# A mixture-of-experts tail: token list written in parts and loaded from POOL's queue, expert tables read two ahead, a tile of its own for the second norm

## Chip, cores and metric

One core of a Trainium2 chip. The metric is device time in microseconds (us) of the whole kernel, the median of three runs. The engines are TensorE (PE; its weight loads are PEld), VectorE (DVE), ScalarE (ACT), GpSimd (POOL) and SyncE (SP), each with its own instruction queue, worked through in order. SP and POOL also issue the DMA transfers; all indirect ones (rows gathered or scattered by a list of indices) are POOL's.

## The reference

One layer of a decoder with 2048 tokens of 1024 channels in fp32. First a token mixer (two kinds of attention, gates, an output projection) and a layer norm, which the change does not touch. Then the mixture of experts:

```python
idx, gates = group_route(x2d, w_router, router_bias)   # one of 8 groups of 4 experts; top 2 in it
h = jax.nn.silu(xb @ w_gate[e]) * (xb @ w_up[e])       # per expert: 1024 -> 512
yb = h @ w_down[e]                                     # 512 -> 1024
y = segment_sum(yb * gate, token)                      # two experts per token
out = layer_norm(alpha * x + y, ln2_g, ln2_b)          # the second norm
```

## The kernel before

**Up to the experts.** The mixer writes the normed rows x1 and alpha times x1 (into `scr["y"]`) to DRAM. `route` (L600) gives each token its group and two experts and scatters (token, gate) pairs into a table `scr["tab"]`, one stretch of rows for each expert (L669). `sort_experts` orders the 32 experts so that each of 32 static slots knows how many rows it must hold: wide slots hold 128 + 64 rows, narrow ones 128. `MIX` (L32) is that order by (group rank, expert rank in the group), `BIG` says which slots are wide (14 of 32), `STAGE` which of five parts of `MIX` a slot is in.

**One expert** (`experts`, L946, loop L972). In iteration i the code emits, in this order: `start(i + 1)`, i.e. `prep` of the next expert; the loads of the second norm that fall due; `gate_up(i)`; `hidden(i)`; the norms of the loaded rows; `down(i - 1)`.
- `prep` (L802) reads the expert's table with SP (L808, and L810 for the 64 rows), gathers the token rows `xg` with POOL (L815; tag Z, three buffers), transposes them on TensorE (L823, L831) and splits them into a high and a low part on ScalarE and VectorE (L83, L84). The wide part's result, `x3`, lies in one of two halves of a tile of tag R.
- `weights` (L836) loads 1 MB with SP (L839; staging tag V, five buffers) and splits it (L83, L84) into `wh` and `wl`, tag X. Each expert has four such loads for gate and up and two for down.
- `gate_up` (L847), `hidden` (L872) and `down` (L900) are the three steps of matmuls. `down` scales by the gate (L915), makes the wide part's `y3` on ScalarE and VectorE (L923, L924; tag Y, two buffers) and adds the rows into `scr["y"]` by an indirect DMA that accumulates, on POOL (L927).

**The token list.** `token_list` (L717), emitted at i = 1, works out for each token its place in an order by group and scatters the 2048 token numbers there, sixteen indirect DMAs of 128 rows of 8 bytes on POOL (L756). SP then loads the list into `lst` (L763).

**The second norm.** A 128-token block of that list can be normed once the groups it holds have been summed. Blocks 0 to 12 are normed inside the loop: `when` (L967) gives blocks 0 to 2 to iterations 10, 12, 14, blocks 3 to 6 to 18, 20, 22, 24, blocks 7 to 10 to 26 to 29 and blocks 11 and 12 to 30 and 31. `norm_load` (L992) gathers the rows with POOL (L996) into `fz`, tag Y, shared with `y3`; `norm` (L1013) computes mean and variance (L1019, L425), the inverse root with three Newton steps (`rstd`, L405; products L416, L420), and L1022 and L1023; `norm_rows` stores by POOL (L1008). The last three blocks follow the loop (L988), each with a Newton chain of its own; the first of them takes its passes on ScalarE.

**What sets the order.** The tile framework's planner orders each engine's queue by readiness in its own timing model and by emission order; it puts a wait where a buffer or a result is needed. An engine never passes a waiting instruction, so the table read of SP stands behind its weight loads, and POOL's gathers, y sums, norm loads and stores stand in one line.

Of the kernel before, what the change touches and what calls it, by code (L numbers as in the profile page):

```python
# [11 lines left out]
F32 = mybir.dt.float32  # L12
# [41 lines left out]
class Layer:  # L54
# [662 lines left out]
    def token_list(self):  # L717
# [27 lines left out]
        g = self.b([128, 4, 16])  # L745
# [8 lines left out]
        prev = []  # L754
        for t in range(16):
            st = nc.gpsimd.indirect_dma_start(  # L756
                out=self.scr["list"], out_offset=bass.IndirectOffsetOnAxis(ap=dst[:, t:t + 1], axis=0),
                in_=self.tok[:, t, :], in_offset=None)
            for p in prev:
                self.tc.declare_no_dep(st.ins, p.ins, reason="rows of another token")  # L760
            prev.append(st)
        self.lst = self.c("lst", [128, 16, 2], I32, "binT")
        nc.sync.dma_start(self.lst, self.scr["list"].rearrange("(b p) v -> p b v", p=128))  # L763
# [38 lines left out]
    def prep(self, e, row, big):  # L802
# [8 lines left out]
        S["tb"] = tb  # L811
        xr = []
# [13 lines left out]
        if big:  # L826
            x3 = self.x3s[:, self.turn % 2]
            self.turn += 1
            pt = self.p("aT", [128, KD, 64])
            for k in range(KD):  # L830
                nc.tensor.transpose(pt[:, k, :], xr[1][:, k * 128:(k + 1) * 128], self.ident[0:64, 0:64])  # L831
            self.split(pt, x3[:, :, 0, :], x3[:, :, 1, :])
            S["x3"] = x3
# [112 lines left out]
    def experts(self):  # L946
# [5 lines left out]
        def start(i, e=None):  # L952
            e = expert(i) if e is None else e
            S = self.prep(e, e * ROWS + ROWS, BIG[i])
            S["slot"] = i
            return S

        self.gb = self.norm_consts(2)
        self.x3s, self.turn = self.t("R", [128, 2, KD, 2, 64], F32R, "x3"), 0
        e = expert(0)  # L960
        w = [self.weights("w_gu", e, 0, after=self.fence(self.scats[-1]))]
        cur, nxt, old = start(0, e), start(1), None
        w.append(self.weights("w_gu", e, 1, after=nxt["read"], sync=False))
        w.append(self.weights("w_gu", e, 2, after=self.fence(nxt["gather"])))
        cur["w"] = w
        self.sums, self.reads, self.rows = [], [], []
# [5 lines left out]
        for i in range(32):  # L972
            if i:
                nxt = start(i + 1) if i < 31 else None
            rows = [self.norm_load(b, q) for q, b in when.get(i, ())]
            self.gate_up(cur)
            self.hidden(cur)
            for r in rows:
                self.norm_rows(r, "D")
            if old is not None:  # L980
                self.down(old)
            old, cur = cur, nxt
            if i == 1:
# [20 lines left out]
    def norm_rows(self, r, how):  # L1004

        z, at = r
        self.norm(z, how)
# [5 lines left out]
    def norm(self, x, how):  # L1013
        nc = self.nc
        g, b = self.gb[:, 0, :], self.gb[:, 1, :]
        if how == "D":
            st = self.small([128, 2, 6])
            for h in range(2):
                nc.vector.bn_stats(st[:, h, :], x[:, h * 512:(h + 1) * 512])  # L1019
            mean, var = self.moments(st)  # L1020
            rs = self.rstd(var)
            nc.vector.scalar_tensor_tensor(x, x, mean, g, op0=OP.subtract, op1=OP.mult)  # L1022
            nc.vector.scalar_tensor_tensor(x, x, rs, b, op0=OP.mult, op1=OP.add)  # L1023
            return
        y = self.t("F", [128, D], F32, "fy")
        sm = self.small([128, 5])
        nc.scalar.activation(y, x, AF.Copy, accum_out=sm[:, 0:1])
        nc.vector.tensor_scalar(sm[:, 1:2], sm[:, 0:1], -1.0 / D, None, op0=OP.mult)
        nc.scalar.activation(y, x, AF.Square, bias=sm[:, 1:2], accum_out=sm[:, 2:3])
        nc.vector.tensor_scalar(sm[:, 3:4], sm[:, 2:3], 1.0 / D, None, op0=OP.mult)  # L1030
        rs = self.rstd(sm[:, 3:4])
        nc.vector.tensor_tensor(sm[:, 4:5], sm[:, 1:2], rs, op=OP.mult)
        nc.scalar.activation(x, x, AF.Identity, bias=sm[:, 4:5], scale=rs)
        nc.vector.tensor_tensor(x, x, g, op=OP.mult)  # L1034
        nc.vector.tensor_tensor(x, x, b, op=OP.add)  # L1035

    def finish(self, out):
# [11 lines left out]
        with tc.For_i(0, again, 1) as i:  # L1049
            z = self.t("Y", [128, D], F32, "fz")  # L1050
            nc.sync.dma_start(z, self.scr["y"][ds(i * 128, 128)])
            self.norm(z, "D")
# [133 lines left out]
```

## Time and profile before

| | |
|---|---|
| median of 3 runs | 2571.21 us (2567.74 to 2575.26) |
| the profiled execution | 2575.09 us |
| its span, first to last instruction | 2573.1 us |
| mean granted TensorE clock | 0.974 |
| TensorE matmul busy | 94% of the span |
| VectorE / ScalarE / POOL busy | 73% / 55% / 34% |

The clock is a share of 2.4 GHz. A line of a timeline gives start, duration, engine, line of the kernel, operation, output and inputs; in brackets stands how long the engine had been idle before it and what ended that.

### The profile page before, as it was taken

How to read it: one execution, taken by the hardware profiler on the slowest of the kernel's cores; microseconds unless marked ns; L12 is line 12 of the kernel's file. 1: busy time of each engine (PE TensorE's matmuls, PEld its weight loads, DVE VectorE, ACT ScalarE, POOL GpSimd, SP SyncE). 2: the span in 40 equal slices, each digit the busy share in tenths (PEclk: the TensorE clock that was granted, in tenths of full speed). 3: DMA queues.
4: the chain of work that ended last, by engine and by line, in shares of the span. 5: the costliest groups of instructions: out<-in, count | busy, mean ns of one | idle time of the engine just before them, and what ended most of it. 6: DMA issues, size and time to landing. Idle time of an engine off the chain costs nothing. (4 is left out here: it accounts for less than half of the span.)

```text
span 2573.1 us, 37165 instructions
## 1 busy us (share of the span) xinstructions
PE 2419.9 (94%) x12706; PEld 2032.2 (79%) x12706; DVE 1867.2 (73%) x3065; ACT 1419.6 (55%) x2388; POOL 869.0 (34%) x942
## 2 busy tenths in 40 slices
PE   8999899999999999999999999949979989999992
PEld 7888778988888888888878888737768878877871
DVE  4554757657777877778867878766767877897893
ACT  3442636457776766777732222225656666666661
POOL 0220424234444444444410312232532452332522
PEclk9999999999999999999999999969989999999996
DMA  7747576454443423238274554258699999999993
GB/s 255 202 145 224 158 207 191 154 157 137 138 136 103 152 85 97 86 90 286 92 249 161 189 164 148 92 171 299 220 338 325 354 312 328 325 363 340 349 308 86
DMA packets 173055, 528.52 MB, mean 205 GB/s; under 512 B 28592, under 2 KB 53168, under 8 KB 146096
## 3 DMA queue, kind: packets, MB, share of 16 engines
q1 hardware_dynamic: 155264, 468.38, 53.9%
q0 software_dynamic: 17600, 57.73, 8.5%
q8 instruction: 103, 1.69, 0.3%
q14 instruction: 88, 0.72, 0.1%
HBM read 404.88 MB, written 121.73 MB: 205 GB/s over the span
## 5 line engine op out<-in xcount | busy, mean ns | idle before, releaser
L84 DVE TENSOR_TENSOR wl<-ws,wh 128x2048 fp32r<-128x2048 f32 (+2 forms) x250 | 507.5, 2039 | 148.2 <-ACT wh L83 110.1
L83 ACT ACTIVATE wh<-ws 128x2048 fp32r<-128x2048 f32 (+2 forms) x250 | 424.2, 1713 | 133.6 <-PE pz L865 53.3
L348 POOL TENSOR_TENSOR s<-s,keep 128x512 f32<-128x512 f32 (+2 forms) x320 | 315.3, 991 | 402.4 <-DVE keep L346 401.3
L160 PE MATMUL pmm<-xh,wh 128*128 128x512 f32 x912 | 364.2, 400 | 6.0 <-ACT xh L83 5.8
L161 PE MATMUL pmm<-xl,wh 128*128 128x512 f32 x912 | 362.9, 398 | 0.2 <-DVE xl L84 0.2
L162 PE MATMUL pmm<-xh,wl 128*128 128x512 f32 x912 | 362.9, 398 | 0.2 <-DVE wl L84 0.2
L346 DVE TENSOR_TENSOR_SCAN keep<-pz,keep,s 128x512 f32<-128x512 f32 x192 | 244.9, 1279 | 57.5 <-ACT pz L341 57.0
L84 DVE TENSOR_TENSOR at<-paT,at 128x512 fp32r<-128x512 f32 (+3 forms) x384 | 225.2, 614 | 76.7 <-ACT at L83 74.4
L83 ACT ACTIVATE at<-paT 128x512 fp32r<-128x512 f32 (+3 forms) x384 | 191.4, 541 | 110.8 <-PE paT L351 104.6
L279 POOL TENSOR_SCALAR sw<-sw,st 128x256 f32<-128x256 f32 (+1 forms) x128 | 124.1, 985 | 361.2 <-DVE st L277 163.8
L927 POOL DMA_INDIRECT scr_y<-y,tb x46 | 120.3, 2615 | 289.8 <-ACT y L915 241.7
L160 PEld LDWEIGHTS pmm<-xh,wh 128*128 128x128 f32 x912 | 173.4, 190 | 37.9 <-ACT xh L83 6.2
L340 ACT ACTIVATE s<-pz 128x512 f32<-128x512 f32 (+2 forms) x320 | 172.1, 538 | 54.8 <-PE pz L244 45.2
L162 PEld LDWEIGHTS pmm<-xh,wl 128*128 128x128 f32 x912 | 173.1, 190 | 33.2 <-DVE wl L84 0.5
L161 PEld LDWEIGHTS pmm<-xl,wh 128*128 128x128 f32 x912 | 173.1, 190 | 32.5 <-DVE xl L84 1.0
L859 PE MATMUL pmm<-wh,xt 128*128 128x512 f32 x512 | 178.3, 403 | 4.5 <-ACT h L875 3.0
L243 PE MATMUL pz<-kt,qt 128*128 128x256 f32 (+3 forms) x448 | 164.7, 378 | 13.6 <-DVE keep L346 5.7
L869 PE MATMUL pmm<-wl,xt 128*128 128x512 f32 x512 | 174.5, 400 | 2.5 <-DVE wl L84 2.5
L861 PE MATMUL pmm<-wh,xt 128*128 128x512 f32 x512 | 174.1, 398 | 0.0
L341 ACT ACTIVATE pz<-pz 128x512 f32<-128x512 f32 (+2 forms) x320 | 173.7, 543 | 0.0
L358 PEld LDWEIGHTS po<-at,vt 128*128 128x128 f32 x1152 | 159.9, 190 | 16.4 <-ACT at L83 1.6
L358 PE MATMUL po<-at,vt 128*128 128x256 f32 x1152 | 165.5, 283 | 2.2 <-ACT at L83 1.2
(295 smaller groups left out, 5352.2 us busy)
## 6 DMA issues: line engine op xcount, KB each, us to landing
ws<-in_w_gu SPq DMA_DIRECT2D x128, 1024.0 KB, 8.1
ws<-in_w_dn SPq DMA_DIRECT2D x64, 1024.0 KB, 8.8
ws<-in_w_in SPq DMA_DIRECT2D x57, 512.0 KB, 4.7
qt<-scr_qkh SPq DMA_DIRECT2D x64, 256.0 KB, 5.6
qt<-scr_qkl SPq DMA_DIRECT2D x64, 256.0 KB, 6.5
scr_gate<-sg SPq DMA_DIRECT2D x64, 256.0 KB, 3.1
bs<-in_w_br SPq DMA_DIRECT2D x32, 512.0 KB, 4.0
gl<-scr_gate SPq DMA_DIRECT2D x64, 256.0 KB, 3.8
```

What stands on the lines that cost most here:

```text
L83: nc.scalar.activation(hi, src, AF.Copy)
L84: (lo_eng or nc.vector).tensor_tensor(lo, src, hi, op=OP.subtract)
L160: ins.append(nc.tensor.matmul(ps, wh[:, k, :], h, start=k == 0, stop=False))
L161: ins.append(nc.tensor.matmul(ps, wh[:, k, :], l, start=False, stop=False))
L162: ins.append(nc.tensor.matmul(ps, wl[:, k, :], h, start=False, stop=k == KD - 1))
L341: nc.scalar.activation(z[:, :w], z[:, :w], AF.Sigmoid, scale=-0.125)
L346: nc.vector.tensor_tensor_scan(kp[:, k0:k0 + w][:, ::-1], z[:, :w][:, ::-1], s[:, :w], init, op0=OP.mult, op1=OP.bypass)
L348: nc.gpsimd.tensor_tensor(s[:, :w], s[:, :w], kp[:, k0 + 1:k0 + w + 1], op=OP.mult)
L358: nc.tensor.matmul(o, vt[:, 4 * c + i, :], at[:, r, i], start=(c == top and i == nbs[1] - 1 and r == 0), stop=(c == 0 and i == 0 and r == 1))
L859: nc.tensor.matmul(ps[u], xh, wh[:, kk, u, :], start=a, stop=False)
L861: nc.tensor.matmul(ps[u], xl, wh[:, kk, u, :], start=False, stop=False)
L869: nc.tensor.matmul(ps[u], xh, wl[:, kk, u, :], start=False, stop=z)
```

## The change

The order of stages 1 and 2 alternates groups strictly. The list is scattered in four parts, in iterations 2 to 5, from a tile of its own (`where`, in the place of `bwr`), and loaded by POOL. The table reads of `prep` become a function `read` that runs two experts ahead. `x3` moves to tag Y, and `fz` of the loop becomes one tile that is used by all blocks (tag R, where `x3` was). `norm` takes a list of blocks and makes one Newton chain for all of them; the last three blocks go through it together and are stored after it.

```diff
-       ((1, 0), (7, 0), (7, 1), (1, 1), (7, 2), (1, 2), (1, 3), (7, 3)),
-       ((2, 0), (5, 1), (2, 1), (2, 2), (5, 0), (2, 3), (5, 2), (5, 3)),
+       ((1, 0), (7, 0), (1, 1), (7, 1), (1, 2), (7, 2), (1, 3), (7, 3)),
+       ((2, 0), (5, 1), (2, 1), (5, 2), (5, 0), (2, 2), (5, 3), (2, 3)),
...
-        g = self.b([128, 4, 16])
+        g = self.c("where", [128, 3, 16], F32, "bwr")
...
-        prev = []
-        for t in range(16):
+        self.where, self.lists = dst, []
+
+    def token_rows(self, t0):
+        dst, prev = self.where, self.lists
+        for t in range(t0, t0 + 4):
             st = nc.gpsimd.indirect_dma_start(
...
+        if t0 < 12:
+            return
         self.lst = self.c("lst", [128, 16, 2], I32, "binT")
-        nc.sync.dma_start(self.lst, self.scr["list"].rearrange("(b p) v -> p b v", p=128))
+        nc.gpsimd.dma_start(self.lst, self.scr["list"].rearrange("(b p) v -> p b v", p=128))
...
-            x3 = self.x3s[:, self.turn % 2]
-            self.turn += 1
+            x3 = self.t("Y", [128, KD, 2, 64], F32R, "x3")
...
-        self.x3s, self.turn = self.t("R", [128, 2, KD, 2, 64], F32R, "x3"), 0
+        self.fz = self.t("R", [128, D], F32, "fz")
         e = expert(0)
...
-        cur, nxt, old = start(0, e), start(1), None
+        cur, nxt, old = start(0, read(0, e)), start(1, read(1)), None
...
+        far = read(2)
...
             if i:
-                nxt = start(i + 1) if i < 31 else None
+                nxt = start(i + 1, far) if i < 31 else None
+                far = read(i + 2) if i < 30 else None
...
             if i == 1:
                 self.token_list()
+            if 2 <= i < 6:
+                self.token_rows(4 * (i - 2))
...
-        for r, how in zip(rows, "ADD"):
-            self.norm_rows(r, how)
+        self.norm([z for z, _ in rows], "ADD")
+        for r in rows:
+            self.norm_store(r)
...
-    def norm_load(self, b, stage, tag="Y"):
-        z = self.t(tag, [128, D], F32, "fz")
+    def norm_load(self, b, stage, tag=None):
+        z = self.t(tag, [128, D], F32, "fz") if tag else self.fz
...
+        mv = self.small([128, n, 2])
+        for i, (x, how) in enumerate(zip(xs, hows)):
...
+        rs = self.rstd(mv[:, :, 1], n)
+        for i, (x, how) in enumerate(zip(xs, hows)):
...
```

## Rows read from the trace of the kernel before

**Rows 1.** Busy time by stretch: PE, PEld, DVE, ACT, POOL, PEclk, DMA share, GB/s

```profile
1840.00:1860.00 20.00, 20.00 (x91) 16.51 (x90) 19.12 (x14) 15.01 (x14) 18.17 (x7) 1.00 0.54 159
1860.00:1880.00 20.00, 7.18 (x34) 5.08 (x33) 0.00 (x0) 1.54 (x1) 6.66 (x6) 0.83 0.94 222
...
1900.00:1950.00 50.00, 50.00 (x238) 40.79 (x237) 36.50 (x28) 34.40 (x34) 18.21 (x8) 1.00 0.88 315
```

**Rows 2.** TensorE's timeline, expert stage: the instructions behind its longer idle stretches

```profile
1868.21 0.63 PE L823 MATMUL paT<-ident,xg 128*128 128x128 f32 x4 [3.51 <-DMA xg<-scr_x,tb]
...
1880.43 0.80 PE L912 MATMUL po<-wh,ht 128*128 128x512 f32 x1 [9.74 <-ACT wh L83]
...
1882.75 0.80 PE L914 MATMUL po<-wl,ht 128*128 128x512 f32 x1 [1.10 <-DVE wl L84]
...
2115.15 0.87 PE L823 MATMUL paT<-ident,xg 128*128 128x128 f32 x3 [6.04 <-DMA xg<-scr_x,tb]
...
2307.40 1.22 PE L869 MATMUL pmm<-wl,xt 128*128 128x512 f32 x2 [2.46 <-DVE wl L84]
...
2523.41 0.77 PE L912 MATMUL po<-wh,ht 128*128 128x512 f32 x1 [7.62 <-DVE y L924]
```

**Rows 3.** Busy time by stretch, columns as in rows 1, behind the longest gap

```profile
1880.00:1884.00 4.00, 2.47 (x5) 1.56 (x6) 3.40 (x2) 3.42 (x5) 1.73 (x1) 0.50 1.02 424
1884.00:1888.00 4.00, 4.00 (x15) 3.06 (x15) 4.00 (x4) 3.94 (x4) 0.00 (x0) 0.65 1.00 416
```

**Rows 4.** POOL's timeline: the first, a long and the last list scatter, and the next gather

```profile
1826.37 0.99 POOL L756 DMA_INDIRECT scr_list<-tok,B  x1 [11.72 <-DVE C L777]
...
1842.73 7.49 POOL L756 DMA_INDIRECT scr_list<-tok,B  x1 [0.30 <-issue]
...
1857.57 2.56 POOL L756 DMA_INDIRECT scr_list<-tok,B  x1 [0.30 <-issue]
1860.43 0.97 POOL L815 DMA_INDIRECT xg<-scr_x,tb  x1 [0.30 <-PE pmm L861]
```

**Rows 5.** SP's waits after 1700 us (total, times, longest), and its timeline

```profile
SPq L763 <- DMA scr_list<-tok,B: 18.7, 1, 18.7
...
1864.27 0.39 SPq L763 DMA_DIRECT2D lst<-scr_list  x1
```

**Rows 6.** POOL's timeline: a wide expert's two gathers, 128 rows and 64 rows

```profile
1780.99 0.94 POOL L815 DMA_INDIRECT xg<-scr_x,tb  x1 [23.19 <-DMA tb<-scr_tab]
1782.34 0.90 POOL L815 DMA_INDIRECT xg<-scr_x,tb  x1 [0.41 <-PE paT L889]
```

**Rows 7.** VectorE's timeline beside the long list scatter

```profile
1842.70 6.67 DVE L84 TENSOR_TENSOR wl<-ws,wh 128x2048 fp32r<-128x2048 f32 x3
```

**Rows 8.** POOL's waits after 1700 us: total, times, longest

```profile
POOL xg L815 <- DMA tb<-scr_tab: 85.3, 9, 23.2
```

**Rows 9.** ScalarE's timeline near the end

```profile
2521.95 1.08 ACT L923 ACTIVATE y<-po 64x512 f32<-64x512 f32 x2 [8.36 <-DMA out<-fz,lst]
```

**Rows 10.** POOL's timeline: loads and stores of norm blocks 4, 7 and 11

```profile
2225.42 1.30 POOL L996 DMA_INDIRECT fz<-scr_y,lst  x1 [7.58 <-DMA out<-fz,lst]
...
2357.02 2.61 POOL L996 DMA_INDIRECT fz<-scr_y,lst  x1 [6.42 <-DMA scr_y<-y,tb]
...
2399.75 2.78 POOL L1008 DMA_INDIRECT out<-fz,lst  x1 [0.80 <-DMA tb<-scr_tab]
...
2494.82 3.20 POOL L996 DMA_INDIRECT fz<-scr_y,lst  x1 [6.67 <-issue]
...
2517.12 0.97 POOL L1008 DMA_INDIRECT out<-fz,lst  x1 [0.73 <-DVE sm L416]
```

**Rows 11.** DMA issues after 1700 us: times, median us from issue to landing

```profile
out<-fz,lst POOLq DMA_INDIRECT x16, 10.4
```

**Rows 12.** POOL's timeline: its last instruction

```profile
2561.69 0.95 POOL L1008 DMA_INDIRECT out<-fz,lst  x1 [0.30 <-issue]
```

**Rows 13.** VectorE's groups after 2540 us: busy, mean ns

```profile
L416 DVE SCALAR_TENSOR_TENSOR sm<-sm 128x1 f32<-128x1 f32 x9 | 1.8, 213 | 0.0
```

More of the change, by code (lines that the diff above doesn't have):

```diff
@@ L753, in token_list @@
         v.tensor_reduce(self.late[:, 0:1], late[0:1], axis=AX.X, op=OP.add)
-        prev = []
-        for t in range(16):
+        self.where, self.lists = dst, []
+    def token_rows(self, t0):
+        nc = self.nc
+        dst, prev = self.where, self.lists
+        for t in range(t0, t0 + 4):
             st = nc.gpsimd.indirect_dma_start(
@@ L800, in overflow_list, with read @@
         v.tensor_copy(self.ove, po)
-    def prep(self, e, row, big):
+    def read(self, e, row, big):
         nc = self.nc
@@ L811, in prep @@
         S["tb"] = tb
+        return S
+    def prep(self, e, row, big, S=None):
+        nc = self.nc
+        S = self.read(e, row, big) if S is None else S
+        tb = S["tb"]
         xr = []
@@ L950, in expert, with read, start @@
             return nc.sync.value_load(self.eid[0:1, i:i + 1], min_val=0, max_val=31)
-        def start(i, e=None):
+        def read(i, e=None):
             e = expert(i) if e is None else e
-            S = self.prep(e, e * ROWS + ROWS, BIG[i])
+            S = self.read(e, e * ROWS + ROWS, BIG[i])
             S["slot"] = i
             return S
+        def start(i, S):
+            return self.prep(None, None, BIG[i], S)
         self.gb = self.norm_consts(2)
-        self.x3s, self.turn = self.t("R", [128, 2, KD, 2, 64], F32R, "x3"), 0
+        self.fz = self.t("R", [128, D], F32, "fz")
         e = expert(0)
         w = [self.weights("w_gu", e, 0, after=self.fence(self.scats[-1]))]
-        cur, nxt, old = start(0, e), start(1), None
+        cur, nxt, old = start(0, read(0, e)), start(1, read(1)), None
         w.append(self.weights("w_gu", e, 1, after=nxt["read"], sync=False))
@@ L1004, in norm_rows, with norm_store @@
     def norm_rows(self, r, how):
+        self.norm([r[0]], how)
+        self.norm_store(r)
+    def norm_store(self, r):
         z, at = r
-        self.norm(z, how)
         st = self.nc.gpsimd.indirect_dma_start(out=self.io["out"], out_offset=at, in_=z, in_offset=None)
@@ L1011, in norm_rows, with norm @@
         self.rows.append(st)
-    def norm(self, x, how):
+    def norm(self, xs, hows):
         nc = self.nc
+        n = len(xs)
         g, b = self.gb[:, 0, :], self.gb[:, 1, :]
[L1016 to L1035, printed above, removed]
@@ new lines, in norm @@
+        mv = self.small([128, n, 2])
+        for i, (x, how) in enumerate(zip(xs, hows)):
+            if how == "D":
+                st = self.small([128, 2, 6])
+                for h in range(2):
+                    nc.vector.bn_stats(st[:, h, :], x[:, h * 512:(h + 1) * 512])
+                nc.vector.bn_aggr(mv[:, i], st)
+            else:
+                y = self.t("F", [128, D], F32, "fy")
+                sm = self.small([128, 3])
+                nc.scalar.activation(y, x, AF.Copy, accum_out=sm[:, 0:1])
+                nc.vector.tensor_scalar(sm[:, 1:2], sm[:, 0:1], -1.0 / D, None, op0=OP.mult)
+                nc.scalar.activation(y, x, AF.Square, bias=sm[:, 1:2], accum_out=sm[:, 2:3])
+                nc.vector.tensor_scalar(mv[:, i], sm[:, 0:3:2], 1.0 / D, None, op0=OP.mult)
@@ new lines, in norm @@
+        rs = self.rstd(mv[:, :, 1], n)
+        for i, (x, how) in enumerate(zip(xs, hows)):
+            m, q = mv[:, i, 0:1], rs[:, i:i + 1]
+            if how == "D":
+                nc.vector.scalar_tensor_tensor(x, x, m, g, op0=OP.subtract, op1=OP.mult)
+                nc.vector.scalar_tensor_tensor(x, x, q, b, op0=OP.mult, op1=OP.add)
+            else:
+                nm = self.small([128, 1])
+                nc.vector.scalar_tensor_tensor(nm, m, -1.0, q, op0=OP.mult, op1=OP.mult)
+                nc.scalar.activation(x, x, AF.Identity, bias=nm, scale=q)
+                nc.vector.tensor_tensor(x, x, g, op=OP.mult)
+                nc.vector.tensor_tensor(x, x, b, op=OP.add)
@@ L1051, in finish @@
             nc.sync.dma_start(z, self.scr["y"][ds(i * 128, 128)])
-            self.norm(z, "D")
+            self.norm([z], "D")
             nc.sync.dma_start(out[ds(i * 128, 128)], z)
```

## The prediction

> **What bounds the kernel now.** I read the windows by stretch first. From 1900 us on TensorE is busy without a break at full clock (50.00 of 50 us), with the 16 DMA engines at 0.88 and POOL at 18.21 of 50 [rows 1]. So the expert stage is bound by TensorE wherever nothing stops it, and what the change can win is TensorE's idle time and the tail behind it. The exception is 1860 to 1880 us, where TensorE works 7.18 of 20 us; just before it, the DMA engines fall to 0.54 and POOL is busy 18.17 of 20 us [rows 1].
>
> Next, TensorE's own timeline gives its idle stretches with what ended them [rows 2]: 3.51 us for a late token gather, 9.74 us for a down-projection weight, 1.10 us for its low half, later 6.04 us for another late gather, 2.46 us for a weight half, and 7.62 us near the end for y3, the small block's output. After an idle stretch the clock is granted at 1.2 GHz: 0.50 in the four us after the 9.74 us gap and 0.65 in the next four [rows 3]. Busy time times missing clock gives the price: 2.47 x 0.50 + 4.00 x 0.35 = 2.6 us.
>
> POOL's timeline then says why the gather was late. The sixteen scatters that write the token list run in one row from 1826.37 to 1857.57 + 2.56 = 1860.13, 33.8 us, and the gather goes out right behind, at 1860.43 [rows 4]. SP's rows say why the weight was late: its load of the list waited 18.7 us for the scatters and went out at 1864.27, 4.1 us after the last of them had been issued; all weight loads stood behind it [rows 5], and the 9.74 us are TensorE's wait for such a weight. Two queues thus gave one stall.
>
> **The change part by part.**
>
> *List in four parts, list load on POOL.* Removed from the path: 3.51 + 9.74 + 1.10 = 14.35 us idle and 2.6 us of slow clock, 17.0 us. The scatters stay, 33.8/16 = 2.1 us each, 8.4 us for a part. POOL has some 32 of 50 us free [rows 1], which hides them; without that cover they would again stand ahead of a gather. The load itself is late to nobody: the first reader of the list comes iterations later. But POOL now waits for the last scatters, 4.1 us, and makes the load's 2048 pieces of 8 bytes. No row shows such a load on POOL. The nearest rows: SP issued it in 0.39 us [rows 5]; a scatter of 128 such pieces, the first, takes 0.99 us, sixteen like it 15.8 us [rows 4]; a gather takes 0.94 us for 128 rows and 0.90 for 64 [rows 6], so 64 pieces more cost 0.04 us and 2048 pieces 0.9 + 1.3 = 2.2 us. I take 2.2 us, because the two gathers measure the very slope that is asked for; the ends are 0.39 and 15.8. Behind the waiting load stand gathers and y scatters. Their cover: a POOL row of 33.8 us delayed TensorE by just 3.51 us, so 30.3 us were hidden; 8.4 + 4.1 + 2.2 = 14.7 us fit. Cost nothing.
>
> One scatter took 7.49 us, not 0.99. It starts at 1842.73 [rows 4] as VectorE starts three wide subtractions in a row (1842.70, 6.67 us [rows 7]) and ends 0.85 us after them: POOL stood still while VectorE worked, and lost 6.5 us. A load on POOL that meets such a run loses as much: 14.7 + 6.5 = 21.2 us still fit into 30.3. [...]
>
> *Tables two experts ahead.* POOL waited 85.3 us for tables [rows 8], but TensorE's rows blame a gather only for the 3.51 us, counted above, and the 6.04 us. Whether a table or POOL's order made the second late, its row does not say. Gain between 0 and 6.04 + 2.6 = 8.6 us; I take 0, since POOL has other waits in the same places. SP issues as many table reads as before, one expert earlier.
>
> *Y tiles and the second norm's own tile.* At the end ScalarE waited 8.36 us for y3's buffer, until an output store of the norm had landed [rows 9]; that is TensorE's 7.62 us. With the norm out of Y this goes, and so does the slow clock behind it, which I put at the 2.6 us worked out above: 10.2 us. The two x3 buffers join y3 in Y; as wide experts now alternate with narrow ones, an x3 takes the buffer of the y3 two experts back, and no wait is added.
>
> The norm pays for it: with one tile, block b+1's load waits on POOL until block b's store has landed. From a load to the store behind it POOL's rows take 22.3 us (2494.82 to 2517.12) at best and 42.7 us (2357.02 to 2399.75) at worst [rows 10], and a store lands in 10.4 us [rows 11]: a block every 32.7 to 53.1 us, where blocks 7 to 12 come one an expert. From 2357.02 six blocks at the best pace have the last store out at 2357.0 + 5 x 32.7 + 22.3 = 2542.8 us. Before, the last store of all went out at 2561.69 [rows 12]; 10.2 us less for y3 and 1.2 for the batched norm below put it at 2550.3 on the same clock (the 17.0 us move both). So the chain fits by 7.5 us, and I add the 2.9 us by which one landing of 10.4 exceeds that. A wait like it, 7.58 us on POOL [rows 10], left TensorE without a gap, so in mid-stage I count none. The ends are 0 and the rival below.
>
> *One Newton chain for the last three blocks.* The nine Newton products took 1.8 us of VectorE [rows 13]; three chains become one, so two thirds go, 1.2 us, of 0 to 1.8. The batch must wait for all three loads; the chain already ends with the third block, so this adds nothing.
>
> *Order.* Each expert costs the same. Experts 13 to 15 are now three narrow ones in a row, and weights are asked for fastest there. The one such run of before ended in the 2.46 us gap [rows 2]. Bounds 0 and 2.46 + 2.6 = 5.1 us; I take 2.5, the gap as it stands. Sums into the same rows now alternate; no row shows POOL waiting for such a sum, so nothing.
>
> **Sum.** -17.0 - 10.2 - 1.2 + 2.9 + 2.5 = -23.0 us. The profiled execution took 2575.1 us (span 2573.1), 3.9 us above the median, so it would come to 2552; from the median of 2571.2 I forecast 2548 us. A measurement of this kernel can tell about 0.3%, 7.7 us, from no change.
>
> **Rivals.**
> *The second late gather goes too*: tables no longer hold POOL up. For it, the 85.3 us [rows 8]; against it, POOL's order stays. 8.6 us more: 2540 us. Chance 0.14.
>
> *The list still gets in the way*: the planner may issue all scatters together, since all their rows are known at once, and the load at its high end stands behind the last part. 8.4 + 4.1 + 15.8 + 6.5 = 34.8 us of POOL against 30.3 hidden leaves 4.5 us and 2.6 of clock: 2555 us. The scatters in one row cost their 3.51 + 2.6, nearly the same. [...] Chance 0.15.
>
> *The norm's wait replaces y3's at the end*: the 10.2 us are not won: 2558 us. For it, six loads in consecutive experts on one tile. Chance 0.14.
>
> *Slower: the norm's single tile sets the pace.* In the last six experts each load blocks POOL until a store lands, with y sums and gathers behind it. At the mean of both ends, 42.9 us a block, block 12's store goes out at 2357.0 + 5 x 42.9 + 22.3 = 2593.8, that is 43.5 us past 2550.3. Without the 2.9 us the sum is 2545.3, so this gives 2589 us. It decides where 2545.3 has grown by 33.6 us, to 2578.9: at (2550.3 + 33.6 - 2379.3)/5 = 40.9 us a block. For it, the slow pair [rows 10]; against it, the fast pair, and that norms that are late find VectorE free at the end. Chance 0.14.
>
> **How the numbers follow.** Forecast 0.43. Low end: forecast without the two added costs and with the second gather won and the whole 1.8: 2548 - 5.4 - 8.6 - 0.6 = 2533. High end: 2558 with the dear run of narrow experts (2.6) and the list's 7.1: 2568. It leaves out the slow rival. Two small ones together may end within 0.3%: 0.09. Slower 0.13, faster 0.78.
>
> **What would show it.** Right: no TensorE gap near 1865 to 1883 and clock 1.00 there; list scatters in groups with gathers between; SP never waiting for the list; no ScalarE wait for a store before y3; POOL's load waiting for an output store once a block. Wrong: a DMA wait of the second norm's load on POOL over 10 us with TensorE idle behind it after 2350 us, or VectorE waiting there for the norm's tile.

## The result, and the profile after

| | before | after |
|---|---|---|
| median (lowest to highest), us | 2571.21 (2567.74 to 2575.26) | 2599.46 (2591.62 to 2605.44) |
| ratio to before, 95% interval | 1 | 1.0107 [1.0057, 1.0156] |
| profiled execution, us | 2575.1 | 2599.46 |
| its span, us | 2573.1 | 2597.6 |
| TensorE's first transpose of gathered tokens, us | 1727.62 | 1732.67 |
| from there to the start of the last matmul ("the experts"), us | 803.5 | 819.0 |
| from there to the end of the span ("the tail"), us | 42.0 | 45.9 |

The change makes the kernel 1.07% slower, some 27 us, and the interval, 0.57 to 1.56%, is clear of no change; forecast was 2548 us. Up to the first transpose both kernels issue the same instructions in the same order; that row lies between 1726 and 1739 us in the profiles of this study, so its 5 us are no effect of the change. The loss is 15.5 us in the experts and 3.9 us in the tail. In the experts TensorE's trace has 3533 matmuls in both kernels; it works 763.6 us before and 767.0 after, and stands idle for 40.3 and 52.4 us. Experts and tail are used as two measures from here on.

TensorE's busy time by stretch (columns: PE, PEld, DVE, ACT, POOL, PEclk, DMA share, GB/s), first before, then after:

```profile
1800.00:1900.00 100.00, 85.24 (x396) 68.17 (x395) 64.16 (x82) 54.19 (x54) 43.00 (x25) 0.93 0.80 265
1900.00:2000.00 100.00, 100.00 (x475) 81.45 (x474) 76.17 (x58) 71.47 (x68) 35.87 (x15) 1.00 0.93 324
2000.00:2100.00 100.00, 98.87 (x469) 80.31 (x468) 87.99 (x95) 70.87 (x65) 52.29 (x14) 1.00 0.96 343
...
2200.00:2300.00 100.00, 100.00 (x474) 81.95 (x473) 86.57 (x89) 70.43 (x67) 32.39 (x18) 1.00 0.98 343
```

```profile
1800.00:1900.00 100.00, 84.25 (x378) 66.59 (x377) 65.52 (x85) 54.05 (x52) 47.68 (x28) 0.91 0.78 249
1900.00:2000.00 100.00, 95.64 (x437) 76.96 (x436) 70.80 (x53) 63.29 (x60) 23.37 (x11) 0.97 0.82 287
2000.00:2100.00 100.00, 91.15 (x423) 74.16 (x422) 73.83 (x81) 62.42 (x58) 40.24 (x16) 0.95 0.93 334
...
2200.00:2300.00 100.00, 94.51 (x433) 76.61 (x432) 80.72 (x81) 65.42 (x59) 37.51 (x15) 0.97 0.94 329
```

The stretch with the list stall, 1800 to 1900, has not improved, and three stretches that ran full or nearly so before now have holes. TensorE's timeline after shows them, where [rows 2] showed six others:

```profile
1832.78 0.74 PE L872 MATMUL pmm<-wh,xt 128*128 128x512 f32 x2 [2.52 <-ACT wh L83]
...
1877.34 1.22 PE L872 MATMUL pmm<-wh,xt 128*128 128x512 f32 x2 [11.28 <-ACT wh L83]
...
1952.09 1.22 PE L872 MATMUL pmm<-wh,xt 128*128 128x512 f32 x2 [3.95 <-ACT wh L83]
...
2011.48 1.11 PE L902 MATMUL paT<-ident,h 128*128 128x128 f32 x4 [7.80 <-DVE sm L413]
...
2209.92 1.22 PE L880 MATMUL pz<-wl,x 128*128 128x512 f32 x2 [5.21 <-DVE wl L84]
...
2396.78 0.80 PE L934 MATMUL po<-wh,h 128*128 128x512 f32 x1 [3.84 <-DVE y L937]
```

Gone are the 7.62 us for y3 and the 6.04 us for a gather near 2115. In their place stand 17.75 us for weights (the first three) and 16.85 us behind VectorE (the last three). Ahead of each of these three, VectorE's timeline shows it standing at the norm's statistics for a load that had not landed:

```profile
2007.79 1.29 DVE L1046 BATCH_NORM_STATS2 sm<-fz 128x6 f32<-128x512 f32 x2 [8.84 <-DMA fz<-scr_y,lst]
...
2206.39 1.29 DVE L1046 BATCH_NORM_STATS2 sm<-fz 128x6 f32<-128x512 f32 x2 [6.71 <-DMA fz<-scr_y,lst]
...
2393.06 1.29 DVE L1046 BATCH_NORM_STATS2 sm<-fz 128x6 f32<-128x512 f32 x2 [6.47 <-DMA fz<-scr_y,lst]
```

The waits after 1700 us name the causes (total, times, longest), first of SP, then of ScalarE, VectorE and POOL:

```profile
SPq L815 <- DMA scr_y<-y,tb: 117.1, 11, 30.7
SPq L817 <- DMA scr_y<-y,tb: 92.1, 10, 15.9
...
ACT wh L83 <- DMA ws<-in_w_gu: 87.6, 26, 15.9
...
DVE sm L1046 <- DMA fz<-scr_y,lst: 42.2, 7, 11.6
...
POOL xg L829 <- DMA tb<-scr_tab: 31.9, 4, 9.7
POOL fz L1017 <- DMA out<-fz,lst: 24.6, 5, 7.2
```

SP waits 209 us in front of table reads (L815 and L817) until a y sum has landed; before, that was one wait of 4.2 us. VectorE waits 42.2 us at the norm's statistics for a load that has not landed (before 2.5 us, 2 times), and POOL 24.6 us in front of norm loads for a store to land. POOL's wait for tables has fallen from 85.3 us [rows 8] to 31.9. How the first comes about can be read near 1870 us, from POOL's timeline, then SP's, then ScalarE's:

```profile
1853.98 5.36 POOL L761 DMA_INDIRECT scr_list<-tok,where  x1 [0.30 <-issue]
1859.64 0.96 POOL L761 DMA_INDIRECT scr_list<-tok,where  x1 [0.30 <-issue]
1860.90 1.61 POOL L940 DMA_INDIRECT scr_y<-y,tb  x1 [0.30 <-ACT h L888]
1862.82 1.44 POOL L940 DMA_INDIRECT scr_y<-y,tb  x1 [0.31 <-DVE gu L895]
1865.74 1.24 POOL L770 DMA_DIRECT2D lst<-scr_list  x1 [1.48 <-DMA scr_list<-tok,where]
...
1869.98 0.33 SPq L815 DMA_DIRECT2D tb<-scr_tab  x1
1870.57 2.06 SPq L852 DMA_DIRECT2D ws<-in_w_gu  x4
...
1875.37 1.91 ACT L83 ACTIVATE wh<-ws 128x2048 fp32r<-128x2048 f32 x1 [13.68 <-DMA ws<-in_w_gu]
```

The scatters were not spread: fourteen stand in a row from 1829.34, one gather follows, then the other two. The y sums stand behind them on POOL. A y sum scatters by the indices in its expert's table, so it holds that table's buffer until it has landed; the read two experts ahead needs that buffer, SP waits 30.7 us for it, and four weight loads stand behind the read on SP. They go out at 1870.57 in one burst. TensorE's 11.28 us are this wait: the stall of [rows 5] has come back on the same queue, through another wait.

The norm's chain is read on POOL: the loads of blocks 6 and 10, the store of block 10, the loads of blocks 11 and 12, and, out of TensorE's timeline, the last matmul:

```profile
2334.48 2.88 POOL L1017 DMA_INDIRECT fz<-scr_y,lst  x1 [6.62 <-DMA out<-fz,lst]
...
2489.09 0.98 POOL L1017 DMA_INDIRECT fz<-scr_y,lst  x1 [4.49 <-DMA out<-fz,lst]
...
2530.32 6.65 POOL L1032 DMA_INDIRECT out<-fz,lst  x1 [0.31 <-issue]
2540.16 0.99 POOL L1017 DMA_INDIRECT fz<-scr_y,lst  x1 [3.20 <-DMA out<-fz,lst]
...
2556.70 1.00 POOL L1017 DMA_INDIRECT fz<-scr_y,lst  x1 [0.30 <-issue]
...
2551.68 0.39 PE L927 MATMUL po<-wl,ht 128*128 128x512 f32 x1
```

From block 6 to block 10 a block takes (2489.09 - 2334.48)/4 = 38.7 us, and block 11 follows after 51.1; the prediction had taken 32.7. Block 12 is loaded 5 us after TensorE's last matmul has begun; before, at 2500.21, that was 31 us ahead of it.

### The profile page after: what moved, and what is told of

Read it like the earlier page. It is cut to its first block, busy times and chain, and to the rows that moved or that the text cites. A ratio compares the mean times of both kernels' runs of the same rounds, so it can differ in the third digit from the quotient of the medians.

```text
span 2597.6 us, 37155 instructions
## 1 busy us (share of the span) xinstructions
PE 2428.8 (94%) x12706; PEld 2036.3 (78%) x12706; DVE 1869.9 (72%) x3048; ACT 1420.6 (55%) x2388; POOL 848.9 (33%) x943
## 5 line engine op out<-in xcount | busy, mean ns | idle before, releaser
L940 POOL DMA_INDIRECT scr_y<-y,tb x46 | 126.7, 2754 | 309.8 <-ACT y L928 254.3
L872 PE MATMUL pmm<-wh,xt 128*128 128x512 f32 x512 | 175.4, 409 | 23.7 <-ACT wh L83 17.7
L874 PE MATMUL pmm<-wh,xt 128*128 128x512 f32 x512 | 170.9, 401 | 0.0
```

The lines of the kernel that those rows point to most:

```text
L872: nc.tensor.matmul(ps[u], xh, wh[:, kk, u, :], start=a, stop=False)
```

## The experiments

All runs stand beside runs of the kernel before on the same chip, and the ratio is to these. Experts and tail are those of the one profiled execution, which can lie up to 8 us from the run's median (e1: 2595.0 against 2587.1 us). "Halves": the norm's tile has two halves used in turn. "Tied": the norm's first statistics are placed behind an instruction of their expert. "Tied parts": each part's scatters are placed behind the last y sum before them in the code.

| run | list | table reads, buffers | norm tile | ratio [95%] | experts, us | tail, us |
|---|---|---|---|---|---|---|
| (after) | parts | two ahead, 8 | single | 1.0107 [1.0057, 1.0156] | 819.0 | 45.9 |
| e1 | parts | two, 16 | single | 1.0034 [1.0021, 1.0046] | 783.4 | 70.4 |
| e2 | parts | two, 16 | halves | 0.9978 [0.9968, 0.9987] | 785.5 | 47.6 |
| e3 | as before | two, 8 | as before | 1.0001 [0.9991, 1.0010] | 806.8 | 42.1 |
| e4 | parts | as before | as before | 0.9991 [0.9981, 1.0001] | 797.2 | 43.2 |
| e5 | parts | one, 8 | single | 1.0091 [1.0066, 1.0115] | 789.6 | 70.4 |
| e7 | parts | two, 8 | as before | 1.0015 [1.0000, 1.0029] | 806.9 | 42.8 |
| e8 | tied parts | two, 16 | halves | 0.9977 [0.9960, 0.9994] | 785.9 | 47.4 |
| e9 | tied parts | two, 16 | halves, tied | 0.9875 [0.9853, 0.9896] | 759.1 | 47.2 |
| e10 | parts | two, 8 | single, tied | 1.0121 [1.0105, 1.0136] | 799.2 | 69.7 |
| e11 | as before | as before | as before, tied | 0.9968 [0.9958, 0.9978] | 792.3 | 42.2 |
| e12 | parts | two, 16 | halves, tied | 0.9897 [0.9882, 0.9911] | 761.3 | 46.4 |
| e13 | tied parts | one, 8 | halves, tied | 0.9909 [0.9895, 0.9923] | 772.2 | 44.8 |
| e14 | as before | as before | single | 0.9988 [0.9970, 1.0006] | 782.7 | 57.2 |
| e15 | parts | two, 8 | single, two blocks in Y | 1.0132 [1.0107, 1.0157] | 832.0 | 46.2 |
| e16 | parts | two, 8 | halves | 1.0064 [1.0046, 1.0083] | 817.2 | 44.6 |
| e17 | before, with the new order of experts alone | | | 1.0011 [0.9998, 1.0023] | 806.1 | 42.2 |
| e18 | e9 with the old order of experts | | | 0.9862 [0.9846, 0.9878] | 760.2 | 46.2 |
| e19 | as before | as before | halves, tied | 0.9912 [0.9896, 0.9928] | 775.9 | 42.3 |

**e1 and e2: after, with sixteen table buffers, then also two halves.**

```diff
-        tb = [self.sb.tile(..., tag="tb", bufs=8) ...]
+        tb = [self.sb.tile(..., tag="tb", bufs=16) ...]
...
-        self.gc = self.c("gc", [128, 96])
+        self.gc = self.c("gc", [128, 96], F32, "ji")
...
-        self.fz = self.t("R", [128, D], F32, "fz")
+        self.fzs, self.turn = self.t("R", [128, 2, D], F32, "fz"), 0
```

The first two pairs of lines are e1 (gc takes the place of a tile that is done with, for room), all three e2, where norm_load takes the halves in turn.

> The changed kernel with sixteen table buffers instead of eight (the group constants move into a dead tile to make room). Theory A (a table read two ahead waits on SP for the y sum of an older expert to give up its buffer, and the weight loads stand behind it): SP's waits of table reads for scr_y fall from 209 us to under 20, the 11 us gap near 1877 us and the other gaps that end with a weight go, and the time falls from 2599 to 2555 to 2575 us. Theory B (the single norm tile is the cause): waits for scr_y may go, the time stays at 2590 to 2600 us.

> As the one before, and the norm inside the loop alternates between two halves of its tile. Theory A alone: the same time as with sixteen buffers, within 5 us. Theory B: at least 10 us less than that kernel, and POOL's norm loads no longer wait for an output store (24.6 us in the changed kernel). Both together: 2540 to 2555 us.

Measured: 1.0034 and 0.9978. In time e1, 2587.1 us, lies between the ranges of its two theories; e2 is 15.7 us faster than e1, as theory B had it, but not at the 2540 to 2555 us of both together. In e1 SP's waits for y sums at the table reads are gone and the experts are 35.6 us shorter, but the tail is 24.5 us longer. POOL's timeline of e1, its last loads through the single tile and the last matmul:

```profile
2520.19 0.99 POOL L1017 DMA_INDIRECT fz<-scr_y,lst  x1 [1.94 <-DMA out<-fz,lst]
...
2545.00 0.96 POOL L1017 DMA_INDIRECT fz<-scr_y,lst  x1 [6.02 <-DMA out<-fz,lst]
...
2558.95 0.96 POOL L1017 DMA_INDIRECT fz<-scr_y,lst  x1 [2.62 <-DMA out<-fz,lst]
...
2522.92 0.39 PE L927 MATMUL po<-wl,ht 128*128 128x512 f32 x1
```

These are blocks 10 to 12; from block 7, at 2389.05, to block 10 each took 43.7 us. With the last matmul 29 us sooner than in after, these three still go one behind the other, each behind a landed store. With two halves (e2) the tail is 47.6 us again. So the tables' buffers cost time in the experts, the single tile in the tail, and in after the first hides the second.

**e3 and e4: before, with the table reads two ahead, and with the list's parts and POOL's load.**

```diff
+        far = read(2)
...
-                nxt = start(i + 1) if i < 31 else None
+                nxt = start(i + 1, far) if i < 31 else None
+                far = read(i + 2) if i < 30 else None
```

```diff
+            if 2 <= i < 6:
+                self.token_rows(4 * (i - 2))
...
-        nc.sync.dma_start(self.lst, ...)
+        nc.gpsimd.dma_start(self.lst, ...)
```

> The kernel of before with the table reads two experts ahead and nothing else (eight buffers). Theory A: SP waits over 150 us for y sums at the table reads, and the kernel is slower than before by 15 to 40 us. Theory B: no slower than before, 2560 to 2575 us.

> The kernel of before with the token list in four parts and its load on POOL, nothing else. Both theories: the stall of before near 1865 to 1883 us (14.35 us idle and slow clock) goes and the time is 2550 to 2562 us. If the scatters still run in one row and a gather stands behind them, the gain is only the weights' share, 2557 to 2565 us.

Measured: 1.0001 and 0.9991. e3 is no slower, as theory B had it, although the waits of theory A came; e4 misses both of its ranges. In e3 the waits are there, and the stall as well (SP's waits, then TensorE's timeline):

```profile
SPq L810 <- DMA scr_y<-y,tb: 103.5, 9, 14.8
SPq L808 <- DMA scr_y<-y,tb: 92.4, 12, 17.0
...
1869.78 1.22 PE L866 MATMUL pmm<-wh,xt 128*128 128x512 f32 x2 [11.90 <-ACT wh L83]
```

But it stands where the list's stall stood before and takes its place; the experts are 3.3 us longer, no more. The two late gathers of [rows 2], 3.51 and 6.04 us, are not in e3, so its zero is a loss and a gain that cancel. In e4 the list no longer stops SP, and a table read does, for 22.6 us, behind a y sum that left POOL only at 1867.00, after the row of scatters; a gather costs TensorE 4.61 us. Part of the stall is won (797.2 against 803.5 us), and in the median it cannot be told from nothing.

**e5 and e7: after, with one part taken back each**, the distance of the reads in e5 (`far` goes, `start(i + 1, read(i + 1))`), the norm's place in e7:

```diff
-        self.fz = self.t("R", [128, D], F32, "fz")
+        self.x3s, self.turn = self.t("R", [128, 2, KD, 2, 64], F32R, "x3"), 0
...
-        z = self.t(tag, [128, D], F32, "fz") if tag else self.fz
+        z = self.t(tag or "Y", [128, D], F32, "fz")
```

> Everything of the change but the table distance: rows are read one expert ahead again, through the eight buffers. Theory A (the reads two ahead wait for y sums because eight buffers are too few, some 18 us of the loss): SyncE's wait for y sums at the table reads falls from 209 us to under 30, and the time comes out as with sixteen buffers, a ratio of 1.001 to 1.005 to the kernel before. Rival (sixteen buffers helped by something else, and the distance itself is not the cost): the ratio stays at 1.008 to 1.013.

> Everything of the change but the place of the norm's tile: it comes from the shared pool with y3 again, and the gathered second tile from its two halves. Theory N (the single norm tile costs some 14 us by itself: loads wait for stores, VectorE stands at the statistics): the ratio falls from 1.011 to 1.004 to 1.007, SyncE's wait for y sums stays near 200 us, and the wait of y3 for the pool near the end is back at 7 to 9 us of PE. Rival (the two losses overlap, so that one mended alone brings little while the table reads wait): 1.008 to 1.012.

Measured: 1.0091 and 1.0015. e5 lies in its rival's range and cannot be told from after. In e5 SP's waits for y sums fell to 20 us as theory A says, and the experts to 789.6 us, but the tail is 70.4 us as in e1: the time is not won, because the single tile takes it (blocks 10 to 12 are loaded at 2519, 2545 and 2559 us, as in e1). So the rival's reason, that the distance is not the cost, does not follow from its range. e7 fell further than expected, with SP's waits still there (218 us) and y3's gap back (6.89 us): against the place it had before, the norm's new one costs 0.92%, some 24 us (10 to 37 by the intervals).

**e8 and e9: e2, with each part's scatters placed behind the y sum of its expert; in e9 also the norm's first statistics behind ht's subtraction.**

```diff
+            self.tc.add_manual_dep(st.ins, self.sums[-1][1].ins.name, NOSYNC, reason="order")
...
-        self.split(pt, ht[:, 0], ht[:, 1])
+        self.hm = self.split(pt, ht[:, 0], ht[:, 1])
...
-                    nc.vector.bn_stats(st[:, h, :], x[:, h * 512:(h + 1) * 512])
+                    o = nc.vector.bn_stats(st[:, h, :], x[:, h * 512:(h + 1) * 512])
+                    if late:
+                        self.tc.add_manual_dep(o.ins, self.hm.ins.name, NOSYNC, reason="order")
```

> Sixteen table buffers and two halves for the norm's tile as in the second run, and each part of the list's scatters tied behind the y sum of its own expert, so that four stand on POOL at a time. Theory L (the scatters stand in a row in every kernel so far, and what stands behind them, y sums and gathers, is what takes back the list's gain): the y sums of the third and fourth expert leave POOL some 15 us earlier, and the time falls by 4 to 10 us against the second run's, a ratio of 0.994 to 0.996. Rival (with sixteen buffers nothing on SyncE waits for these y sums, and PE already runs at 97 us of 100 there, so the row of scatters costs nothing any more): 0.997 to 0.999.

> As the kernel with the list's parts tied, and the norm's first statistics tied behind the subtraction for ht of the same expert, so that VectorE meets them some 20 us after the load leaves. Theory N2 (what is left of the norm's loss is VectorE standing in order at the statistics for a load that has not landed, 20.8 us in eight waits in the second run): these waits fall under 5 us and the time by another 4 to 8 us, a ratio of 0.990 to 0.995. Rival (PE had work during these waits, or the later stores hold the next loads back): the ratio stays within 0.001 of the kernel with the parts tied, or rises.

Measured: 0.9977 and 0.9875. Spreading the scatters adds nothing to e2, as the rival had it. Moving the statistics wins 1.0%, more than expected. VectorE's waits and two stretches, e8, then e9:

```profile
DVE sm L1051 <- DMA fz<-scr_y,lst: 19.2, 8, 3.8
...
2000.00:2100.00 100.00, 96.23 (x448) 78.45 (x448) 83.24 (x88) 66.80 (x65) 46.42 (x16) 0.98 0.94 333
...
2200.00:2300.00 100.00, 93.31 (x432) 74.92 (x431) 87.28 (x104) 65.13 (x60) 42.96 (x17) 0.98 0.93 328
```

```profile
DVE sm L1051 <- DMA fz<-scr_y,lst: 0.8, 1, 0.8
...
2000.00:2100.00 100.00, 100.00 (x475) 81.92 (x474) 90.08 (x91) 73.20 (x69) 39.42 (x16) 1.00 0.97 346
...
2200.00:2300.00 100.00, 98.34 (x467) 80.42 (x466) 87.06 (x89) 71.00 (x66) 42.42 (x18) 1.00 0.99 353
```

VectorE works in order; where it stands for a norm load, as in the three lines of after above, the weight halves and hidden values behind it are late for TensorE.

**e10 and e11: the tied statistics alone, on after and on before.** The edit is e9's without its first line.

> The change as it is (one norm tile, eight table buffers), with the norm's first statistics alone tied behind the subtraction for ht of the same expert. Theory N2 (the single tile costs time because its loads leave late and VectorE, in order, stands at the statistics until they land): VectorE's 42 us at the statistics fall under 10 and the time falls by 15 to 30 us, a ratio of 0.999 to 1.005. Rival N3 (the single tile costs by its chain, store before load, which pushes blocks into the tail or makes POOL stand; a later reader makes that chain longer): 1.007 to 1.015.

> The kernel before, with the norm's first statistics tied behind the subtraction for ht of the same expert and nothing else. Theory N2: there VectorE stands only 2.5 us at the statistics, so there is next to nothing to win: 0.997 to 1.002. Rival (a later place for the norm's work is worth 1% in any kernel, whatever it waits for): 0.985 to 0.993.

Measured: 1.0121 and 0.9968. In e10 the experts shrink by 19.8 us (VectorE's waits 42.2 to 20.1 us) and the tail grows by 23.8 us, with blocks 11 and 12 loaded at 2546.45 and 2560.93: N2's mechanism shows in the experts, though the waits did not fall under 10 us; N3, whose range holds the time, takes the gain back. For e11 N2's range is missed by a hair, within the interval; VectorE's waits there went from 2.5 to 1.1 us only, so most of its gain has another cause. TensorE's timeline shows a part of it: the 6.04 us for the second late gather of [rows 2] are gone. POOL's timeline of before shows why that gather was late:

```profile
2090.06 11.77 POOL L927 DMA_INDIRECT scr_y<-y,tb  x1 [9.82 <-ACT y L915]
2102.14 2.57 POOL L815 DMA_INDIRECT xg<-scr_x,tb  x1 [0.30 <-issue]
```

It waited for no table; it stood behind a y sum that took 11.77 us. In e11 the gather leaves at 2092.49 and TensorE does not wait for it. What else e11 gains by stays open.

**e12 and e13: e9 without the tied parts; e9 with tables one ahead through eight buffers.**

> The fastest kernel so far without the ties of the list's parts: sixteen table buffers, two halves for the norm's tile, statistics tied, the scatters in one row again. If the row of scatters costs nothing once SyncE never waits for a y sum (as the run with the ties alone said), the ratio is 0.986 to 0.990; if the ties had a part in the gain, 0.991 to 0.996.

> The fastest kernel so far with tables read one expert ahead through eight buffers in place of two ahead through sixteen (list parts and statistics tied, two halves for the norm's tile). Theory T (POOL stands some 80 us for tables that are read late, and the late gathers come back): gaps of PE behind gathers of 4 to 12 us and a ratio of 0.991 to 0.996. Rival (the distance and the buffers only mattered through the norm's loads behind them on POOL): 0.986 to 0.990.

Measured: 0.9897 and 0.9909. e12 lies in the first of its two ranges; the 0.2% between e9 and e12 are within the intervals, so no gain of the ties is shown. Reading two ahead through enough buffers brings 0.34%, some 9 us, hardly more than the intervals: in e13 POOL waits 90.4 us for tables, in e9 22.6. Theory T's gaps behind gathers did not come; the one long gap of e13 after 1800 us, 5.82 us, is for h.

**e14 and e15: before with the single tile alone (the reverse of e7's edit); after with blocks 10 and 12 in Y.**

```diff
-            rows = [self.norm_load(b, q) for q, b in when.get(i, ())]
+            rows = [self.norm_load(b, q, "Y" if b in (10, 12) else None) for q, b in when.get(i, ())]
```

> The kernel before with the change's norm tile alone: one tile of its own, the gathered second tile in the pool of y3. Theory P (one tile makes a chain of load, norm, store, landing of about 45 us a block, which is slower than the experts deliver blocks, so that two blocks are left for the tail): the stretch from TensorE's last matmul to the end grows from 42 us to 65 to 75, the experts' own stretch of 803.5 us shrinks by the 5 to 12 us of the y3 wait, and the ratio is 1.004 to 1.012. Rival (the tile's waits hold the experts up): the experts' stretch grows, the tail stays under 55 us.

> The change with blocks 10 and 12 of the second norm in the pool of y3 again, all other blocks in the single tile, eight table buffers. Theory P: the chain is broken where it runs into the tail, so the tail falls from 74 us to 42 to 52 while the experts' stretch stays near 791 us: a ratio of 0.999 to 1.004. Rival (the tail is long for another reason, the batched norm of the last three blocks or the order of the last sums): the tail stays over 60 us and the ratio at 1.006 or more.

(The 74 and 791 us of after in this text, and the 791 in the next, were misread; its trace has 45.9 and 819.0, as in the table.)

Measured: 0.9988 and 1.0132. e14 lies below theory P's range and fits neither P nor the rival. In it POOL waits 50.7 us in eight norm loads for a store, blocks 7 to 10 take 47.6 us each, the tail is 15.2 us longer and the experts 20.8 us shorter; alone, the single tile costs nothing measurable. e15 speaks against theory P as the explanation of after: its tail was not long, and breaking the chain at its end makes the experts of the profile 13 us longer; the ratios of e15 and after differ by 0.25%, within their intervals. Why the experts grow was not found.

**e16: after with two halves, eight buffers** (e2's last two lines).

> The change with two halves for the norm's tile and eight table buffers. Theory A+P: the tail is that of the second run (about 48 us), the SyncE waits for y sums at the table reads stay near 200 us, and the experts' stretch stays near 791 us against the 785.5 of the second run: 0.999 to 1.003. If the table buffers matter only with the single tile: as the second run, 0.996 to 0.999.

Measured: 1.0064, above both ranges, experts 817.2 us, SP's waits for y sums 193 us. Against e2 this prices eight buffers at 0.86% (22 us), clear of the intervals, where the norm's tile is mended; against after it prices the single tile at 0.43% (11 us), which by itself is within the interval of after.

e16 and e7 both have eight buffers and no single tile, and e7, with the norm in Y, is 0.49% faster. In e16 VectorE waits 24.9 us at the statistics and TensorE has gaps behind it of 8.03, 4.70 and 3.74 us, as in after; in e7 the wait is 1.8 us and none of these gaps is there. So they are not the single tile's. They come with the exchange of places (the norm in R, x3 in Y) together with the rest of the change, for e14, the exchange alone, has no gap behind VectorE over 2.5 us. Why was not found.

**e17 and e18: the order of experts**, new in before, and old in e9 (the tuple MIX alone).

> The kernel before with the new order of experts in its second and third row, nothing else. The forecast's term was +2.5 us (0 to 5.1), a ratio of 1.000 to 1.002. Rival (alternating wide and narrow experts evens out the weight loads, the gap before the narrow run goes with its wait): 0.996 to 0.999. A ratio over 1.003 would say that the order takes part in the loss.

> The fastest kernel so far with the old order of experts. If the order costs what the run of the order alone said (0.11%) and the forecast's +2.5 us, this is faster by 2 to 4 us: 0.986 to 0.987; if the order is neutral or good here, 0.987 to 0.989.

Measured: 1.0011 and 0.9862. Both say that the new order costs about 0.1%; neither by itself is clear of no effect. e18 is the fastest kernel of the study, 2540.24 us where before took 2576.09.

**e19: before with two halves and tied statistics**, list, tables and order as before.

> The kernel before with two halves for the norm's tile and the statistics tied behind ht's subtraction; list, tables and order as before. Theory L3 (with the norm out of the way the list's stall of 14 us of PE and 2.6 of clock is still there, and only the parts with POOL's load remove it): a gap of 10 to 15 us near 1880 us and a ratio of 0.993 to 0.996, 3 to 6 us or more above the 0.991 of the kernel with the list in parts, one expert ahead. Rival (the list's stall is taken back later in any kernel): 0.989 to 0.992.

Measured: 0.9912, the rival's range, and equal to e13's 0.9909, though the stall is whole in e19 and gone in e13. Their windows, e19, then e13:

```profile
1800.00:1900.00 100.00, 85.19 (x394) 68.46 (x393) 71.14 (x91) 58.21 (x55) 51.41 (x25) 0.93 0.81 271
1900.00:2000.00 100.00, 100.00 (x477) 81.63 (x476) 72.74 (x57) 67.74 (x64) 34.68 (x14) 1.00 0.92 324
...
2400.00:2500.00 100.00, 98.96 (x464) 80.16 (x463) 93.10 (x112) 68.11 (x63) 37.41 (x16) 1.00 0.95 325
```

```profile
1800.00:1900.00 100.00, 99.56 (x474) 81.24 (x473) 79.61 (x92) 67.13 (x64) 56.18 (x23) 1.00 0.95 309
1900.00:2000.00 100.00, 94.18 (x441) 76.22 (x440) 67.69 (x54) 63.18 (x62) 47.86 (x22) 0.97 0.95 307
...
2400.00:2500.00 100.00, 95.61 (x438) 75.59 (x437) 91.81 (x125) 64.11 (x61) 47.23 (x18) 1.00 0.89 295
```

In e13 TensorE has done 14.4 us more by 1900 and 8.6 us more by 2000, with a wait of 5.82 us for h between; it loses 3.4 more after 2400. The experts end up 3.7 us shorter and the tail 2.5 us longer: most of what the list's parts win is given back within the same kernel (e13 also has the new order, some 0.1%).

## Why the prediction was wrong

Measured against the forecast's -23.0 us is +1.07%, +27.5 us. The difference of some 50 us is read from the ratios of after, e1, e16 and e2 (1% is 25.7 us): sixteen table buffers and two halves take 1.29%, 33 us, off after, and of the 25.9 us that the other parts were to win, e2 shows 5.7. The prediction priced each part alone and added. Alone on the kernel before, the reads (e3), the list (e4), the single tile (e14) and the order (e17) each move the time by 0.12% at most, none clear of no effect; what costs time is how they meet.

- **Tables two experts ahead, taken at 0: the first step that failed.** It said "SP issues as many table reads as before, one expert earlier". It counted the reads and not how long a table's buffer is held: eight buffers, up to two an expert, are taken by the experts read ahead, the two at work, and those whose y sums have not landed. A read that comes earlier then waits on SP, with the weights behind it. The price is 0.73% (after against e1, 0.2 to 1.2 by the intervals) to 0.86% (e16 against e2, 0.65 to 1.07), 19 to 22 us. The bounds, 0 to a gain of 8.6, excluded a loss without a reason. Alone on the kernel before (e3) the reads cost nothing, their wait standing where the list's had stood and both late gathers gone. With sixteen buffers the distance is worth 9 us (e13 to e9).
- **The norm's own tile, +2.9 taken: the second.** "So the chain fits by 7.5 us" rested on the best pace, 32.7 us a block. The 22.3 us behind it are neither the best (block 12 of before takes 19.0, from 2500.21 to 2519.21) nor usual: the thirteen blocks of before's loop take 37.2 us from load to store in the mean, with the landing of 10.4 a block every 47.6 us. Beside working experts the tile takes 38.7 (after), 43.7 (e1) and 47.6 us (e14), around the 40.9 from which the slow rival was said to decide. That rival, 2589 us, is nearest to what was measured, and its mechanism is the one that e1, e5 and e10 show in their tails. After itself is only partly that case: its experts are so late that the chain shows in 3.9 us of tail, so that the number came near is in part luck. The single tile costs 0.43% (after against e16) to 0.56% (e1 against e2, clear of the intervals), 11 to 14 us; against the place that the norm had before it is the 0.92% of e7, where the prediction had -10.2 + 2.9 us for leaving Y. Two blind spots stand behind the term. That VectorE stands in order at the statistics until the late load lands (42.2 us) was in no step of the sum, only among the signs of being wrong; "A wait like it ... left TensorE without a gap" was read from one wait of POOL, not from VectorE's queue. And alone on the kernel before (e14) it costs nothing, since shorter experts pay for the longer tail.
- **List in parts, -17.0.** The mechanism at the place was right where SP was free: in e2 TensorE runs 97.3 of 100 us from 1800 to 1900 against 85.2. In after the stall stayed, through the tables. The scatters went out in one row, as the rival "the list still gets in the way" had it; that rival priced the POOL row at 7 us lost and did not see that SP would wait for the y sums behind it. And where the stall went, much of its gain was given back (e4, e13 against e19). With both losses mended (e2) the change is worth 0.22%, 5.7 us, of the 25.9 forecast for its other parts. Only with the statistics moved as well (e9), an edit that is no part of the change, does it come to 1.25%, 32 us.
- **Right:** y3's gap is gone (-10.2 forecast; its 7.62 us of idle time are not in after, and come back in e7). The second late gather is gone too, as one rival had it, but its 2540 us did not come with it; nor is that rival's reason shown, since the gather stood behind a y sum and is also gone in e11 and e14, which read their tables as before does. POOL's load of the list took 1.24 us, within 0.39 to 15.8, taken as 2.2. It met no wide subtraction of VectorE, while a scatter did (5.36 us at 1853.98, beside two wide subtractions of 4.48 us that began at 1854.00), as in [rows 7].
- **Order, +2.5:** 0.11% and 0.13%, 3 us: right in size as far as the intervals tell. The batched Newton chain (-1.2) is below what can be measured (its 1.8 us were the products of L416 alone; the nine of L420 take another 1.4); from the last load to the end of the span after takes 33.4 us, before 31.3.

Of the signs for right, SP no longer waits for the list and ScalarE not for a store before y3; but the gap is back near 1877 us and the scatters went out in one row. Of the signs for wrong, VectorE stood at the norm's tile after 2350 us (6.47 us at 2393.06, with 3.84 us of TensorE behind it).

Open stay: most of why tied statistics help before (e11) with so little VectorE waiting; why the norm in R, even in halves, brings VectorE to the statistics too soon in the changed kernel; why e15's experts grow; and what share of e9's 1.0% is the wait itself and what its followers.

## What to carry to other kernels

Before reading something earlier, count the buffers by who holds them longest: a table whose indices drive a scatter is held until the scatter has landed, and a load that waits for it on a shared queue holds back every load behind it. A private single buffer for load, compute and store is priced at its pace, with landings, over the last blocks, not at its best block; and a reader on an in-order engine belongs where its load has surely landed, which was worth 1.0% in e9, 0.3% on the kernel before, and nothing where the single tile took it back (e10). Price parts together, and mend losses together: with the reads' distance alone taken back (e5) the experts were 29 us shorter and the time fell by 0.16%, within the noise, because the tail took the rest.

## What was not expected of the hardware

A plain load of 2048 pieces of 8 bytes costs POOL 1.24 us to issue, little more than a gather of 128 rows (0.94 us, [rows 6]). POOL's indirect transfers take longer beside a wide subtraction of VectorE (128x2048, 2.2 us). Of the 40 gathers of before between 1760 and 2500 us, the 13 that met none in their first 0.9 us took 0.99 us at most; the 27 that met one took 2.26 us in the median and up to 9.22. The y sum of 11.77 us ahead of the second late gather stood beside four such subtractions.

And of queues: 196 us of SP's waits for y sums stand in a kernel that is no slower than before (e3), 193 us in one that sixteen buffers make 22 us faster (e16). The total of a queue's wait is no price, only the gaps of TensorE and the tail are.
